# A decoder step on one core: one PSUM bank per unit of the recurrence, earlier decay rows, and key and value weights in 512 KB pieces

## The chip, the core and the metric

The kernel runs on one core of a Trainium2 chip. The core has five engines that run their own queues in order: TensorE (PE in the profile, with its weight loads as PEld), VectorE (DVE), ScalarE (ACT), GpSimd (POOL) and SyncE (SP), which issues nearly all DMA transfers. The metric is device time in microseconds, the median over several executions; lower is better.

## The reference

One inference step of one hybrid decoder layer over 1024 prompt tokens and 8 x 4 sample tokens, all float32, model width 1024. Cut to what matters here:

```python
def hybrid_layer(x, mem_k, mem_v, ssm_h, ...):
    proj = rmsnorm(x, norm_mix) @ w_in                 # z, x/B/C, dt, pool input
    xbc = silu(causal_dwconv(conv_buf, xbc, ...))
    y, ssm_new = ssd_chunked(xs, dt, a, b_ssm, c_ssm, ssm_h)   # 16 heads of 64, state 128
    y = gated_group_rmsnorm(y + xs * ssm_d[:, None], z, ssm_norm)
    pooled = multiscale_pool(...) @ w_pool * pool_scale
    x = x + concat([y, pooled]) @ w_out
    x = x + memory_attention(rmsnorm(x, norm_mem) @ w_mq, mem_k, mem_v) @ w_mo
    return x + conv_gated_mlp(rmsnorm(x, norm_ffn))

def ssd_chunked(x, dt, a, b_in, c_in, h0):             # chunks of 128 tokens
    acs = cumsum(dt * a, within a chunk)
    decay = exp(acs[l] - acs[s]) for s <= l
    y_diag = (C B^T * decay) (x dt)                    # within the chunk
    chunk_states = B^T (exp(acs[-1] - acs) x dt)       # what the chunk adds to the state
    h_next = h * exp(acs[-1]) + chunk_states
    y_off = (exp(acs) C) h                             # from the state before the chunk

def memory_kv(mem, norm_memkv, w_mk, w_mv):            # 256 memory tokens
    hm = rmsnorm(mem, norm_memkv)
    return hm @ w_mk, hm @ w_mv
```

## The kernel before

All prompt and sample tokens (1056 columns) go through each projection together, features on the partitions. Each float32 operand is split into two parts, `hi` and `lo`, and a product is three matmuls (hi x hi, hi x lo, lo x hi). For weights this is done on the fly. A list of `steps` in the order of use loads one piece `[128, 512]` each (256 KB) into a `wr` tile, and `wsplit` makes `wh` on ACT and `wl = wr - wh` on DVE. There are three tiles each of `wr`, `wh` and `wl`. `prep()` runs the next step whenever fewer than two split pieces (units of weights) are ready, and then asks for the loads that stand `AHEAD` = 2 steps further on. A piece is consumed in four blocks of 128 columns.

The stages that matter here follow each other on PE:

1. `w_in`: 28 output tiles, each 8 k-steps of 9 matmuls with 352 columns, into `mm` tiles of three banks (two such tiles, and beside them two `ms` banks of one).
2. In the background of this stage runs the recurrence, a generator that `tick()` advances after each k-step, by one `yield` every `SSD_PACE` = 1.6 ticks (3 at first). Its 32 units are 2 groups x 8 chunks x 2 halves of 4 heads. For a unit, `ssd_load` fetches the decay rows `acs` of its 4 heads, spread over 128 partitions (256 KB), into an `s` tile; `ssd_pre` transposes x into an `ms` bank and multiplies it out into `xd`, and makes `am` (decays times `C B^T`) and `ce` (decayed C) in the tile of the decay rows, by ACT and DVE; `ssd_post`, one unit later, does the output matmuls into an `ms` bank `py` and the state matmul into another `ms` bank `pst`, adds the first to x and the second to the state `hT`. `ssd_group`, once per two units, takes an `ms` bank too. The two `ms` banks are handed out in turn.
3. The samples' recurrence, which loads states `h0T` into `ld` tiles (three tiles of 528 KB), and the pooled half of `w_out` (8 tiles): its inputs come from `scr_pool` through `ld`, and the residual input `xT` is loaded into an `ld` tile for each of the 8 tiles, added and stored to `scr_xp`.
4. Keys and values of the 256 memory tokens: 16 pieces of `w_mk` with 4 x 3 matmuls of 256 columns each, then 16 pieces of `w_mv` with 2 x 3 matmuls of 512 columns each. Meanwhile ACT and DVE finish the gating of the recurrence's output.
5. The recurrence's half of `w_out` (weights `w_out_y`), which loads `scr_xp` into `ld` tiles, and the rest of the layer.

The order of the instructions on each engine is set by a scheduler when the kernel is built, from the program's order and its own idea of durations; at run time each queue is strictly in order. The instructions are recorded through a helper, so the profile has them all at one line, L91 (L92 in the changed kernel), and the names of the tiles tell them apart: `ms<-xd,btm` is the state matmul, `ms<-s,xd` and `ms<-s` are the output matmuls, `ms<-cst,s` the transposes.

Of the kernel before, what the change touches and what calls it, by code (L numbers as in the profile page):

```python
# [10 lines left out]
ALU = mybir.AluOpType  # L11
# [25 lines left out]
VZ = "ppzppzpzpzpzpzzz"  # L37
SSD_EVERY = 3
SSD_PACE = 1.6
SAMPLE_EVERY = 1.5  # L40
GATE_EVERY = 1.5
FOLD_EVERY = 1.2
WINDOWS = (2, 4, 8, 16)
AHEAD = 2
# [34 lines left out]
def body(ctx, tc, A):  # L79
# [20 lines left out]
    V, S, G, PE, DQ = [InOrder(e) for e in (nc.vector, nc.scalar, nc.gpsimd, nc.tensor, nc.sync)]  # L100
# [3 lines left out]
    def dma(out, in_, after=None):  # L104
        d = DQ.dma_start(out, in_)
        after = after or gate[0]
        if after is not None:
            tc.add_manual_dep(d.ins, after.name, NOSYNC, reason="load order")
        return d
# [25 lines left out]
    def pc(name, i, n=1):  # L135
        o = PAR_COLS[name] + i
        return par[:, o:o + n]

    def stile(dt=F32, w=T):
        return sp.tile([P, w], dt, tag="S", name="s")  # L140
# [4 lines left out]
    def ldtile():  # L145
        return lp.tile([P, T], F32, tag="ld", name="ld")
# [4 lines left out]
    def mbtile():  # L151
        return pmm[0].tile([P, 512], F32, tag="mb", name="mb")

    def mstile():
        if pmm[1] is None:
            return mbtile()
        return pmm[1].tile([P, 512], F32, tag="ms", name="ms")
# [15 lines left out]
    steps, sources, issue = [], [], {}  # L173
    ready = deque()
    raws = {}
    at = [0]
# [8 lines left out]
    def load(i):  # L185
        if i in raws:
            return
        src, alloc = sources[i]
        raw = alloc()
        w = 1  # L190
        for d in src.shape[1:]:
            w *= d
        dst = raw[:, :w]
        dma(dst if len(src.shape) == 2 else dst.rearrange("p (k o) -> p k o", k=src.shape[1]), src)
        raws[i] = (raw, w)

    def source(src, step, ahead, alloc=wtile):
        sources.append((src, alloc))
        issue.setdefault(max(0, step - ahead), []).append(len(sources) - 1)
        return len(sources) - 1  # L200
# [8 lines left out]
    def wsplit(raw, w):  # L209
        hi = wp.tile([P, 512], F32R, tag="wh", name="wh")  # L210
        S.activation(hi[:, :w], raw[:, :w], AF.Copy)
        lo = wp.tile([P, 512], F32R, tag="wl", name="wl")
        V.tensor_tensor(lo[:, :w], raw[:, :w], hi[:, :w].bitcast(F32), op=ALU.subtract)
        ready.append((hi, lo, w))

    def plain(i):
        load(i)
        wsplit(*raws[i])

    def plains(srcs):  # L220
        for src in srcs:
            i = source(src, len(steps), AHEAD)
            steps.append(lambda i=i: plain(i))

    def up_part(j, n):
        return A["w_up"][2 * j + 2 - int(n[1]), int(n[2]) - 1]

    def paired(j, names):
# [24 lines left out]
        for n, m, off, alloc in (("s1", "a21", -7, stmp), ("a11", "a11", -4, wtile), ("a21", "a21", -4, stmp),  # L253
                                 ("s4", "a12", 0, stmp), ("a22", "a22", 5, stmp)):
            ids[n] = source(up_part(j, m), n0, -off, alloc)
        for n, x, off in (("s1", up_part(j, "a22"), -5), ("s4", lambda: q["s2"], 1)):
            issue.setdefault(n0 + off, []).append(lambda n=n, x=x: more(n, x))
# [3 lines left out]
        for n in names:  # L261
            if n == "a12":
                plains([up_part(j, "a12")])
            else:
                steps.append(lambda n=n: one(n))

    def down_weights(name, m, c):
        kind = {"t3": 0, "b22": 1, "t1": 2, "t2": 3}
        if name in kind:
# [4 lines left out]
    plains(A["w_in"][m, h] for m in range(28) for h in range(2))  # L274
    plains(scr["wop"][4 * h:4 * h + 4, :, m * P:(m + 1) * P].rearrange("k p o -> p k o")
           for m in range(8) for h in range(2))
    plains(A["w_mk"][m][:, h * 512:(h + 1) * 512] for m in range(8) for h in range(2))
    plains(A["w_mv"][4 * d + k // 2][:, (k % 2) * 512:(k % 2) * 512 + 512] for d in range(2) for k in range(8))
    for nm, n in (("w_out_y", 8), ("w_mq", 8), ("w_mo", 8), ("w_mo", 8), ("w_mo", 7)):
        plains(A[nm][m, h] for m in range(n) for h in range(2))  # L280
    plains(up_part(j, "a12") for j in EARLY)
# [48 lines left out]
    def background(gen, every, bs=bgs):  # L330
        bs.append([gen, 0, every])

    def pace(every):
        if bgs:
            bgs[0][2] = every
# [130 lines left out]
    for b in range(NB):  # L466
        c = slice(b * BW, (b + 1) * BW)
# [205 lines left out]
    for k in range(KT):  # L673
        for pi, x in enumerate((hh[k], hl[k])):
            for b in range(NB):
                PE.matmul(ps[:2 * H, b, :BW], lhsT=wd[:, k].rearrange("p s h -> p (s h)"),
                          rhs=x[:, b * BW:(b + 1) * BW], start=(k == 0 and pi == 0), stop=(k == KT - 1 and pi == 1))
# [12 lines left out]
    def ssd_group(c, g):  # L690
        l = slice(c * P, (c + 1) * P)
        Bf, Cf = xb[8 + g], xb[10 + g]
        ps = mstile()
        PE.transpose(ps[:, 0:P], Bf[:, l], ident)
        PE.matmul(ps[:, P:2 * P], lhsT=Bf[:, l], rhs=Cf[:, l], start=True, stop=True)
        btm = xa.tile([P, P], F32, tag="btm", name="btm", bufs=2)
        S.activation(btm, ps[:, 0:P], AF.Copy)
        cbm = xa.tile([P, P], F32, tag="cbm", name="cbm", bufs=2)
        V.tensor_tensor(cbm, ps[:, P:2 * P], umat, op=ALU.mult)
        grp[g] = (btm, cbm)  # L700

    def ssd_load(c, g, hf):
        h0 = 8 * g + 4 * hf
        at = stile()
        dma(at[:, 0:512].rearrange("p (h l) -> p h l", h=4),
            scr["acs"][h0:h0 + 4, c * P:(c + 1) * P].partition_broadcast(P))
        return at
# [27 lines left out]
    def ssd_post(c, g, hf, am, ce, xd, btm):  # L735
        l = slice(c * P, (c + 1) * P)
        h0 = 8 * g + 4 * hf
        py = mstile()
        for i in range(2):
            o = slice(i * P, (i + 1) * P)  # L740
            for e in range(2):
                PE.matmul(py[64 * e:64 * e + 64, o], lhsT=xd[:, 0, 2 * i + e], rhs=am[:, 2 * i + e],
                          start=True, stop=(c == 0))
            if c > 0:
                for e in range(2):
                    hc = (h0 + 2 * i + e) * 64
                    PE.matmul(py[64 * e:64 * e + 64, o], lhsT=hT[:, hc:hc + 64], rhs=ce[:, 2 * i + e],
                              start=False, stop=True)
        pst = mstile()
        PE.matmul(pst[:, :256], lhsT=btm, rhs=xd[:, 1].rearrange("p h d -> p (h d)"), start=True, stop=True)  # L750
        for i in range(2):
            x = xb[h0 // 2 + i]
            V.scalar_tensor_tensor(x[:, l], x[:, l], pc("ssm_d", h0 // 2 + i), py[:, i * P:(i + 1) * P],
                                   op0=ALU.mult, op1=ALU.add)
        hs = hT[:, h0 * 64:h0 * 64 + 256]
        if c == 0:
            V.tensor_copy(hs, pst[:, :256])
        else:
            hv = hs.rearrange("p (h d) -> p h d", h=4)
            V.tensor_tensor(hv, hv, cd_t[:, c, h0:h0 + 4].unsqueeze(2).to_broadcast([P, 4, 64]), op=ALU.mult)  # L760
            V.tensor_tensor(hs, hs, pst[:, :256], op=ALU.add)
        if c == 7:
            dma(A["o_ssm_p"][:, h0 * 64:h0 * 64 + 256], hs)

# [108 lines left out]
    units = [(c, g, hf) for g in range(2) for c in range(8) for hf in range(2)]  # L873

    def ssd_all():
        loads = {}
        loads[0] = ssd_load(*units[0])
        loads[1] = ssd_load(*units[1])
        yield
        yield  # L880
        pend = None
        for u, un in enumerate(units):
            if un[2] == 0:
                ssd_group(un[0], un[1])
                yield
            nxt = ssd_pre(*un, loads.pop(u))
            yield
            if pend is not None:
                ssd_post(*pend[0], *pend[1])
            if u + 2 < len(units):  # L890
                loads[u + 2] = ssd_load(*units[u + 2])
            yield
            pend = (un, nxt)
        ssd_post(*pend[0], *pend[1])
        yield

    background(ssd_all(), SSD_EVERY)
    for f in XBC_ORDER[6:]:
        xbc_tile(f)
# [43 lines left out]

    pace(SSD_PACE)
    left = {"p": deque(range(8)), "z": deque(range(8))}
    for i, c in enumerate(VZ):
        if "p" not in VZ[i:] and "p" == VZ[i - 1]:
            background(ssd_sample(), SAMPLE_EVERY)
        (pool_tile if c == "p" else z_tile)(left[c].popleft())
# [117 lines left out]
    for d in range(2):  # L1067
        pv = [mbtile() for _ in range(2)]
        for k in range(8):
            whi, wlo, _ = next_unit()  # L1070
            for mt in range(2):
                c = slice(mt * P, (mt + 1) * P)
# [219 lines left out]
    for m in range(8):  # L1292
# [20 lines left out]
        for lb in (1, 0):  # L1313
            src = t[:, lb * 512:(lb + 1) * 512]
# [38 lines left out]
    for c in ATTN:  # L1353
        if c == "s":
            u = len(pts)
# [3 lines left out]
        elif c == "t":  # L1359
            u = len(pt)  # L1360
            pt[u] = attn_tr(pts[u])
        elif c == "o":
            u = min(pt)
# [19 lines left out]
    hs = [None] * 8  # L1383
# [254 lines left out]
    xd = {n: [] for n in xparts}  # L1638
# [108 lines left out]
    for i, name in enumerate(DN_ORDER):  # L1747
# [4 lines left out]
        for m, (c0, c1) in dn_units(name):  # L1752
# [4 lines left out]
            for k in range(c0 // P, c1 // P):  # L1757
# [4 lines left out]
                for b in range(2):  # L1762
                    for pi, (w, h) in enumerate(((whi, 0), (wlo, 0), (whi, TH))):
                        PE.matmul(ps[b][:, :HB], lhsT=w[:, wc], rhs=xt[:, h + b * HB:h + (b + 1) * HB],
                                  start=(first and k == 0 and pi == 0), stop=(k == NH - 1 and pi == 2),
# [14 lines left out]
    xd = xd["b21"]  # L1780
# [3 lines left out]
    for k in range(NH):  # L1784
# [3 lines left out]
        for m in range(4):  # L1788
            wc = slice(m * P, (m + 1) * P)
            for pi, (w, h) in enumerate(((whi, 0), (wlo, 0), (whi, TH))):  # L1790
                PE.matmul(outs[m], lhsT=w[:, wc], rhs=xd[k][:, h:h + LW], start=(k == 0 and pi == 0),
                          stop=(k == NH - 1 and pi == 2))
# [19 lines left out]
    for h in (1, 0):  # L1812
        for i in range(2):
            for m in range(4):
                PE.matmul(o[i][h][:, m * P:(m + 1) * P], lhsT=acc[4 * h + m][:, cs[i]], rhs=ident, start=(m == 0),
                          stop=(h == 1 and m == 3), skip_group_check=True)
# [169 lines left out]
```

## Time and profile before

| | |
|---|---|
| time, median of 3 runs | 1680.94 us (1678.08 to 1685.15) |
| the profiled execution | 1682.67 us, span 1680.9 us |
| granted clock of TensorE | 0.997 |
| PE busy | 1642.8 us (98%) |
| DVE busy | 1180.9 us (70%) |
| ACT busy | 784.4 us (47%) |
| SP's DMA queue, share of 16 engines' span | 54.6%, 289.04 MB |
| moved in all | 306.57 MB, 182 GB/s |

A row of the time line has start and duration in us, engine, operation, the tiles written and read, the shape and a count; in brackets stands how long the engine was idle before, and what ended that. A row of the waits says which engine waited, on what tile, for whom: us in total, times, longest. A row of DMA issues has the count, the size of one, and the median us from issue to landing.

### The profile page before, as it was taken

The page shows a single profiled execution, that of the slowest core. Times are in us where ns is not written, and L with a number is a line of the kernel's source. Part 1 is how long each engine was busy: PE and PEld are TensorE (multiplying, and loading weights), DVE is VectorE, ACT ScalarE, POOL GpSimd, SP SyncE. Part 2 cuts the span into 40 slices and gives each one's busy share as a digit, 9 for nine tenths or more (in the row PEclk, how much of TensorE's full clock was granted, in tenths as well). Part 3 has the DMA queues.
Part 4 walks back from the last instruction along what each step waited for, and adds up shares of the span by engine and source line. Part 5 has one row for each costly group of instructions (what it writes and reads, how often), then busy time and mean ns, then how long its engine had stood idle before and what let it go on. Part 6 is the DMA issues. An engine that isn't in the chain of part 4 may idle for free. (4 is left out here: it accounts for less than half of the span.)

```text
span 1680.9 us, 30585 instructions
## 1 busy us (share of the span) xinstructions
PE 1642.8 (98%) x11808; PEld 1559.3 (93%) x11808; DVE 1180.9 (70%) x1999; ACT 784.4 (47%) x1402; POOL 138.7 (8%) x315
## 2 busy tenths in 40 slices
PE   9999999999999999999999999999999999999998
PEld 8899999899989889999878999999999989999997
DVE  6766768688679576654755896777777878776665
ACT  6565643444514343223533665555544545454451
POOL 0110000001000000000000002232122222100000
PEclk9999999999999999999999999999999999999999
DMA  6243354544696678853666756666566577896542
GB/s 219 85 160 87 66 134 105 111 87 107 224 314 230 192 252 304 301 165 105 233 226 192 228 182 170 177 167 180 145 167 199 168 205 218 284 302 203 159 139 103
DMA packets 187569, 306.57 MB, mean 182 GB/s; under 512 B 43920, under 2 KB 81296, under 8 KB 187424
## 3 DMA queue, kind: packets, MB, share of 16 engines
q1 hardware_dynamic: 178928, 289.04, 54.6%
q0 software_dynamic: 8496, 15.59, 5.6%
q8 instruction: 92, 1.51, 0.4%
q14 instruction: 53, 0.43, 0.1%
HBM read 221.26 MB, written 77.53 MB: 178 GB/s over the span
## 5 line engine op out<-in xcount | busy, mean ns | idle before, releaser
L91 PE MATMUL mb<-s,wh 128*128 128x264 f32 (+4 forms) x4800 | 908.3, 295 | 6.8 <-ACT wh L91 4.7
L91 PEld LDWEIGHTS mb<-s,wh 128*128 128x128 f32 x4800 | 759.5, 189 | 15.1 <-ACT wh L91 5.8
L91 PE MATMUL mb<-s,wl 128*128 128x264 f32 (+4 forms) x2400 | 667.5, 296 | 13.7 <-DVE wl L91 13.3
L91 PEld LDWEIGHTS mb<-s,wl 128*128 128x128 f32 x2400 | 445.8, 189 | 23.6 <-DVE wl L91 20.5
L91 ACT ACTIVATE wh<-wr 128x512 fp32r<-128x512 f32 (+1 forms) x298 | 184.7, 620 | 385.1 <-PE mb L91 177.2
L91 PE MATMUL mm<-s,wh 128*128 128x352 f32 x1728 | 340.9, 330 | 1.5 <-DVE s L91 1.5
L91 PEld LDWEIGHTS mm<-s,wh 128*128 128x128 f32 x1728 | 284.6, 188 | 7.9 <-DVE s L91 2.6
L91 DVE TENSOR_TENSOR wl<-wr,wh 128x512 fp32r<-128x512 f32 (+1 forms) x298 | 201.4, 677 | 109.9 <-ACT wh L91 107.4
L91 PE MATMUL mm<-s,wl 128*128 128x352 f32 x864 | 187.7, 324 | 0.0
L91 DVE SCALAR_TENSOR_TENSOR t<-t,par 128x1104 f32<-128x1104 f32 (+1 forms) x124 | 168.2, 1366 | 26.5 <-ACT t L91 25.4
L91 PEld LDWEIGHTS mm<-s,wl 128*128 128x128 f32 x864 | 147.2, 189 | 1.8 <-issue 1.2
L91 ACT ACTIVATE s<-s 128x512 f32<-128x512 f32 (+7 forms) x117 | 84.2, 730 | 94.2 <-DMA s<-scr_acs 60.7
L91 DVE TENSOR_TENSOR t<-t 128x1024 f32<-128x1024 f32 (+10 forms) x147 | 107.1, 731 | 14.8 <-DMA t<-w_dn 11.1
L91 ACT ACTIVATE wh<-ws 128x512 fp32r<-128x512 f32 x110 | 68.8, 626 | 63.0 <-DMA ws<-w_up 44.9
L91 DVE TENSOR_TENSOR s<-s 128x512 f32<-128x512 f32 (+8 forms) x90 | 74.4, 841 | 30.2 <-ACT s L91 29.8
L91 DVE TENSOR_TENSOR wl<-ws,wh 128x512 fp32r<-128x512 f32 x110 | 75.4, 686 | 21.3 <-ACT wh L91 20.4
L91 ACT ACTIVATE t<-t 128x32 f32<-128x32 f32 (+2 forms) x87 | 46.8, 537 | 88.2 <-DVE t L91 87.7
L91 DVE TENSOR_TENSOR s<-mb,s 128x264 f32<-128x264 f32 (+6 forms) x140 | 61.0, 473 | 30.9 <-PE mb L91 14.9
L91 DVE TENSOR_TENSOR s<-q,s 128x528 fp32r<-128x528 f32 x81 | 56.6, 705 | 36.1 <-ACT s L91 35.7
L91 ACT ACTIVATE t<-t,par 128x1104 f32<-128x1104 f32 (+1 forms) x56 | 73.2, 1307 | 15.5 <-DVE t L91 11.6
L91 ACT ACTIVATE s<-q 128x528 fp32r<-128x528 f32 x81 | 51.9, 643 | 53.7 <-DMA q<-scr_g 50.6
L91 DVE TENSOR_TENSOR ws<-wr,ws 128x512 f32<-128x512 f32 x44 | 30.2, 691 | 57.4 <-issue 31.5
(192 smaller groups left out, 1506.1 us busy)
## 6 DMA issues: line engine op xcount, KB each, us to landing
ws<-w_up SPq DMA_DIRECT2D x88, 256.0 KB, 3.6
q<-scr_g SPq DMA_DIRECT2D x77, 264.0 KB, 3.8
wr<-w_in SPq DMA_DIRECT2D x56, 256.0 KB, 2.9
wr<-w_mo SPq DMA_DIRECT2D x46, 256.0 KB, 3.0
scr_g<-t SPq DMA_DIRECT2D x22, 528.0 KB, 5.2
wr<-w_up SPq DMA_DIRECT2D x44, 256.0 KB, 3.2
s<-scr_acs SPq DMA_DIRECT2D x33, 256.0 KB, 5.1
t<-w_dn SPq DMA_DIRECT2D x32, 256.0 KB, 4.5
```

What stands on the lines that cost most here:

```text
L91: i = fn(*args, **kwargs)
```

## The change

Three edits.

*State part in the output's bank.* `pst` is no longer a bank of its own but the second half of `py`. A unit then takes two `ms` banks where it took three (beside that of `ssd_group`).

*Decay rows four units ahead.* `ssd_load` is called for a unit four units before its use in place of two, and the second half's rows (`hf` = 1) go into an `ld` tile in place of an `s` tile.

*Key and value weights as 512 KB.* `halves` loads a whole `[128, 1024]` row block of `w_mk` or `w_mv` into an `ld` tile, four steps ahead, and splits it in two steps of 512 columns.

```diff
+SSD_AHEAD = 4
...
+    def halves(src):
+        i = source(src, len(steps), 2 * AHEAD, ldtile)
+
+        def half(h):
+            load(i)
+            wsplit(raws[i][0][:, h * 512:(h + 1) * 512], 512)
+
+        steps.extend([lambda: half(0), lambda: half(1)])
...
-    plains(A["w_mk"][m][:, h * 512:(h + 1) * 512] for m in range(8) for h in range(2))
-    plains(A["w_mv"][4 * d + k // 2][:, (k % 2) * 512:(k % 2) * 512 + 512] for d in range(2) for k in range(8))
+    for src in (*(A["w_mk"][m] for m in range(8)), *(A["w_mv"][k] for k in range(8))):
+        halves(src)
...
     def ssd_load(c, g, hf):
         h0 = 8 * g + 4 * hf
-        at = stile()
+        at = ldtile() if (2 * c + hf) % 2 else stile()
...
-        pst = mstile()
-        PE.matmul(pst[:, :256], lhsT=btm, rhs=xd[:, 1].rearrange("p h d -> p (h d)"), start=True, stop=True)
+        pst = py[:, 256:]
+        PE.matmul(pst, lhsT=btm, rhs=xd[:, 1].rearrange("p h d -> p (h d)"), start=True, stop=True)
...
-            V.tensor_copy(hs, pst[:, :256])
+            V.tensor_copy(hs, pst)
...
-            V.tensor_tensor(hs, hs, pst[:, :256], op=ALU.add)
+            V.tensor_tensor(hs, hs, pst, op=ALU.add)
...
-        loads[0] = ssd_load(*units[0])
-        loads[1] = ssd_load(*units[1])
+        for u in range(SSD_AHEAD):
+            loads[u] = ssd_load(*units[u])
...
-            if u + 2 < len(units):
-                loads[u + 2] = ssd_load(*units[u + 2])
+            if u + SSD_AHEAD < len(units):
+                loads[u + SSD_AHEAD] = ssd_load(*units[u + SSD_AHEAD])
```

PE's queue in the recurrence, in the middle of one unit (`ms` with the same number is the same bank in use; in brackets the semaphores that an instruction waits for). Before:

```order
L91 MATMUL ms_2535<-s_2322,xd_2444 64x128 [waits DVE_49]
L91 MATMUL ms_2535<-s_2322,xd_2444 64x128
L91 MATMUL ms_2535<-s_2322,s_1155 64x128 x2
L91 MATMUL ms_2544<-xd_2444,btm_2408 128x256 [waits DVE_49]
L91 MATMUL mm_2416<-s_182,wh_2417 128x352 x3
```

And now:

```order
L92 MATMUL ms_2529<-s_2152,xd_2439 64x128 [waits DVE_49,PE_49]
L92 MATMUL ms_2529<-s_2152,xd_2439 64x128
L92 MATMUL ms_2529<-s_2152,s_1155 64x128 x2
L92 MATMUL ms_2529<-xd_2439,btm_2403 128x256
L92 MATMUL mm_2411<-s_182,wh_2412 128x352 x3
```

The state matmul has lost its wait for DVE: it goes into the bank of the output matmuls.

DVE's queue where it takes up one unit's output (`s_1155` is the state, `dtp` its decay, `par` holds `ssm_d`). Before:

```order
L91 SCALAR_TENSOR_TENSOR s_999<-s_999,par_74,ms_2307 128x128 [waits PE_49]
L91 TENSOR_TENSOR t_2254<-t_2254,t_2244 128x16 [waits DVE_49]
L91 SCALAR_TENSOR_TENSOR s_1152<-s_1152,par_74,ms_2307 128x128
L91 TENSOR_TENSOR s_1155<-s_1155,dtp_92 128x256
L91 TENSOR_TENSOR s_2226<-s_2226,s_549 128x512 [waits Activation_49]
L91 TENSOR_TENSOR s_1155<-s_1155,ms_2316 128x256 [waits DVE_49,PE_49]
```

And now:

```order
L92 TENSOR_TENSOR s_1155<-s_1155,dtp_92 128x256 [waits PE_49]
L92 TENSOR_TENSOR t_2251<-t_2251,t_2241 128x16 [waits DVE_49]
L92 SCALAR_TENSOR_TENSOR s_999<-s_999,par_74,ms_2304 128x128 [waits PE_49]
L92 SCALAR_TENSOR_TENSOR s_1152<-s_1152,par_74,ms_2304 128x128
L92 TENSOR_TENSOR s_1155<-s_1155,ms_2304 128x256 [waits DVE_49]
```

The state's decay stands ahead of the two output additions, and the state's addition no longer waits for PE: the first output addition has waited for both.

SP's queue at the end of the pooled projection. Before:

```order
L91 DMA scr_xp_80<-ld_5322 128x1056 [waits DMAHW4_49,DVE_49]
L91 DMA wr_5435<-w_mk 128x512 [waits DVE_49]
L91 DMA ld_6225<-scr_xp_80 128x1056 [waits DMAHW6_49,DMAHW4_49]
L91 DMA wr_5482<-w_mk 128x512 [waits DMAHW7_49,DVE_49,Activation_49]
L91 DMA scr_xp_80<-ld_5426 128x1056 [waits DMAHW0_49,DVE_49]
L91 DMA wr_5545<-w_mk 128x512 [waits DMAHW1_49,DVE_49,Activation_49]
L91 DMA ld_6337<-scr_xp_80 128x1056 [waits DMAHW2_49,DMAHW0_49]
```

And now:

```order
L92 DMA scr_xp_80<-ld_5292 128x1056 [waits DMAHW4_49,DVE_49]
L92 DMA wr_6029<-w_out_y 128x512 [waits DVE_49]
L92 DMA ld_5396<-xT 128x1056 [waits DMAHW6_49,DMAHW4_49]
L92 DMA wr_6041<-w_out_y 128x512 [waits DMAHW7_49,DVE_49,Activation_49]
L92 DMA scr_xp_80<-ld_5396 128x1056 [waits DMAHW6_49,DMAHW0_49,DVE_49]
L92 DMA ld_5450<-w_mk 128x1024 [waits DMAHW1_49,DMAHW0_49]
L92 DMA ld_5499<-xT 128x1056 [waits DMAHW2_49,DVE_49]
L92 DMA scr_xp_80<-ld_5499 128x1056 [waits DMAHW3_49,DMAHW2_49,DVE_49]
L92 DMA ld_5535<-w_mk 128x1024 [waits DVE_49]
L92 DMA ld_5576<-w_mk 128x1024 [waits DMAHW5_49,DMAHW3_49]
```

The last two `xT` loads now stand between key tiles, the last of them waiting for DVE (the first key tile's splits); pieces of `w_out_y` stand where pieces of `w_mk` stood; and the `scr_xp` loads have left this place.

## The prediction, made before the changed kernel had run

> **What bounds the kernel now.** I read the page's busy shares, then busy time by stretch, the waits of the two stretches that the change touches, and the time line there.
>
> ```profile
> span 1680.9 us, 30585 instructions
> PE 1642.8 (98%) x11808; PEld 1559.3 (93%) x11808; DVE 1180.9 (70%) x1999; ACT 784.4 (47%) x1402; POOL 138.7 (8%) x315
> ```
>
> TensorE (PE) is busy for 98% of the span, so only time in which PE stands can be won: 1680.9 - 1642.8 = 38 us in all. The stretches (us; then busy time and instructions of PE, PEld, DVE, ACT, POOL; clock; DMA share; GB/s) show how much of it lies here:
>
> ```profile
> 195.00:425.00 230.00, 224.53 (x1639) 209.94 (x1638) 176.52 (x374) 93.33 (x165) 5.67 (x19) 1.00 0.48 108
> 440.00:500.00 60.00, 59.47 (x397) 50.99 (x396) 43.19 (x71) 13.86 (x18) 0.00 (x0) 1.00 0.88 297
> 525.00:552.00 27.00, 27.00 (x171) 26.65 (x170) 21.86 (x26) 8.72 (x10) 0.00 (x0) 1.00 0.48 169
> 552.00:604.00 52.00, 48.99 (x304) 41.75 (x303) 34.18 (x57) 23.25 (x36) 0.00 (x0) 1.00 0.62 196
> ```
>
> The recurrence (195 to 425 us) leaves PE idle for 230.0 - 224.5 = 5.5 us, keys and values (552 to 604) for 52.0 - 49.0 = 3.0 us. The other two rows are neighbours that I use below. The clock is full everywhere. In the recurrence the waits are
>
> ```profile
> ACT s L91 <- DMA s<-scr_acs: 62.3, 24, 4.9
> DVE s L91 <- ACT s L91: 36.4, 19, 4.5
> PEld ms L91 <- DVE xd L91: 7.5, 9, 1.8
> PE ms L91 <- DVE xd L91: 5.3, 5, 1.6
> ```
>
> ACT loses 62 us to the decay rows and hands 36 us on to DVE, but only 5.3 us reach PE, in five places, and all of them name `xd`. One of the five:
>
> ```profile
> 216.47 0.38 PE L91 MATMUL ms<-cst,s 128*128 128x128 f32 x2
> ...
> 219.65 0.44 PE L91 MATMUL ms<-s,xd 128*64 128x128 f32 x4
> ...
> 220.29 0.63 ACT L91 ACTIVATE s<-s 128x512 f32<-128x512 f32 x1 [4.93 <-DMA s<-scr_acs]
> ...
> 220.95 0.69 DVE L91 TENSOR_TENSOR s<-s 128x512 f32<-128x512 f32 x1 [4.55 <-ACT s L91]
> 221.56 0.68 DVE L91 TENSOR_TENSOR xd<-ms,dtp 128x512 f32<-128x512 f32 x1
> ...
> 222.30 0.70 PE L91 MATMUL ms<-xd,btm 128*128 128x256 f32 x2 [1.55 <-DVE xd L91]
> ...
> 223.46 0.42 DVE L91 TENSOR_TENSOR s<-s,dtp 128x256 f32<-128x256 f32 x1
> ```
>
> PE transposes the next unit's x at 216.47. DVE could read them out, but stands behind a multiplication that waits for ACT, which waits 4.9 us for decay rows. The state matmul at 222.30 needs no result of this `xd`: its operands are a unit older. It wants the `ms` bank from which this `xd` is read, since there are two such banks and it takes one of its own. So the late load and the third bank per unit make one stall together; either edit alone should end it.
>
> In the stretch of keys and values:
>
> ```profile
> PEld mb L91 <- DVE wl L91: 3.5, 7, 1.0
> PEld mb L91 <- ACT wh L91: 3.0, 3, 1.4
> ```
> ```profile
> PE mb L91 <- ACT wh L91: 2.0, 2, 1.0
> PE mb L91 <- DVE wl L91: 1.0, 3, 0.5
> ```
> ```profile
> ACT wh L91 <- DMA wr<-w_mk: 7.5, 7, 2.9
> ACT wh L91 <- DMA wr<-w_mv: 5.6, 3, 2.7
> ```
>
> PE waits for split weights, and the splits for the 256 KB loads.
>
> **State part in the output's bank: 5.3 us won.** No instruction goes: 32 state matmuls stay, without their wait on DVE. Each `ms` bank is now asked for again one step of the generator later than before. A step takes about what lies between 216.47 and 219.65 above, 3.2 us; `xd` was done at 222.24, 5.8 us after its transposes, and the bank's next user now comes two steps, 6.4 us, after them. So even the late `xd` just fits. What it costs: the two DVE instructions that add `ssm_d` times x to the output now also wait for the state matmul, 0.70 us of PE each (row at 222.30). 32 x 0.70 = 22 us is the most DVE could lose; it has 230.0 - 176.5 = 53 us of idle time there, and the decay of the state (223.46, 0.42 us), which needs neither, is put ahead of them. I take nothing; both ends stay: 0 and, if DVE's lateness reached PE as it did before, 5.3 us of new stalls.
>
> On this the Trainium skill ("PSUM — Partial Sum Buffer", section "PSUM bank collisions raise a hardware error") speaks against the edit: accesses must be kept apart by bank and quadrant, whatever the address, so output and state in one bank wait for each other. The order of the changed program agrees with it (these two wait for the state matmul); by this page alone the sum would be without the 5.3 us.
>
> **Decay rows four units ahead: nothing beyond that.** The same 32 loads, asked for earlier.
>
> ```profile
> s<-scr_acs SPq DMA_DIRECT2D x33, 256.0 KB, 5.1
> ...
> L91 DVE TENSOR_TENSOR xd<-ms,dtp x32: 682/684/692, 149.0 to 410.9; 128x512 f32<-128x512 f32 x32
> ```
>
> A unit takes (410.9 - 149.0) / 31 = 8.4 us, so two more units are 17 us against a landing of 5.1 us: ACT's 62 us and most of DVE's 36 us go. Both engines stay far below PE (93 and 177 of 230 us), so what they win is idle time; it only makes the 5.3 us sure. Every second unit now takes an `ld` tile, so the first state of the samples and the first pooled tiles, which had sat in `ld` from early on, load later, behind the last unit's decay rows. That request and the first split of a pooled tile:
>
> ```profile
> 397.70 0.37 SPq L91 DMA_DIRECT2D s<-scr_acs  x1
> ...
> 428.60 1.07 ACT L91 ACTIVATE s<-ld 128x1056 fp32r<-128x1056 f32 x1
> ```
>
> That leaves 30 us for two waits on a unit's end (8.4 us each) and a load of some 5 us: nothing. Two more activation table loads appear on ACT, hidden by its idle time.
>
> **Key and value weights as 512 KB: 2.0 us won.** 32 loads of 256 KB become 16 of 512 KB; bytes, splits and matmuls stay. What changes is the ring. PE's first two units, and one of the stalls:
>
> ```profile
> 552.38 0.40 PE L91 MATMUL mb<-s,wh 128*128 128x256 f32 x2
> ...
> 553.79 0.40 PE L91 MATMUL mb<-s,wh 128*128 128x256 f32 x2
> ...
> 562.87 2.04 ACT L91 ACTIVATE wh<-wr 128x512 fp32r<-128x512 f32 x3 [2.88 <-DMA wr<-w_mk]
> 563.53 0.69 DVE L91 TENSOR_TENSOR wl<-wr,wh 128x512 fp32r<-128x512 f32 x1 [2.81 <-ACT wh L91]
> ```
>
> A unit is 553.79 - 552.38 = 1.41 us, and three `wr` tiles turn in 4.2 us. Of that the issue takes 0.3 and the two splits 0.7 each (2.04 / 3 and 0.69), so a landing may take 2.5 us; the rows below have 3.3 and 3.0, hence the stalls. Three `ld` tiles of two units each turn in 8.5 us; issue, the second half's wait of 1.41 and its splits take 3.1, so a landing may take 5.4 us.
>
> ```profile
> wr<-w_mk SPq DMA_DIRECT2D x16, 256.0 KB, 3.3
> wr<-w_mv SPq DMA_DIRECT2D x16, 256.0 KB, 3.0
> ld<-h0T SPq DMA_DIRECT2D x8, 512.0 KB, 4.1
> ld<-kc SPq DMA_DIRECT2D x9, 512.0 KB, 6.4
> ld<-xT SPq DMA_DIRECT2D x8, 528.0 KB, 5.0
> scr_xp<-ld SPq DMA_DIRECT2D x8, 528.0 KB, 3.4
> ```
>
> 512 KB lands in 4.1 us (`h0T`) to 6.4 us (`kc`). I take 4.1 to 5: `h0T` is the same form into the same tiles, mostly from 440 to 500 us, where the DMA engines are busier (0.88) than here (0.62). Then the ring keeps pace, and the 3.0 us go. At 6.4 us it would lose (6.4 - 5.4) x 16 / 3 = 5.3 us instead.
>
> The start costs something. `ld` is shared with the last tiles of the pooled projection, and the eighth `xT` load now waits until the first key tile is split:
>
> ```profile
> 546.94 0.69 DVE L91 TENSOR_TENSOR wl<-wr,wh 128x512 fp32r<-128x512 f32 x1 [0.59 <-ACT wh L91]
> 552.57 1.26 DVE L91 TENSOR_TENSOR ld<-mm,ld 128x1056 f32<-128x1056 f32 x1 [4.95 <-PE mm L91]
> 553.75 0.68 DVE L91 TENSOR_TENSOR wl<-wr,wh 128x512 fp32r<-128x512 f32 x1
> ```
>
> The split ends at 547.6, the load lands 5.0 us later near 553, the addition slips by 0.4 us, and the split at 553.75 with it; that one was done at 554.4 and PE wants it two units after 552.38, at 555.2. The fourth key tile waits for the second's splits (two units after 552.38, 555.2) and lands near 560; the fifth waits for the addition's store (554.5 + 3.4) and lands near 562.5. PE wants them at about 561 and 564, less 1.4 us for splitting: 0 to 1 us late each. I charge 1.0 us together, with 0 and 2 as ends. The queue meanwhile holds nothing that PE needs sooner: three tiles of `w_out_y` are asked for earlier than before, in the idle `wr` tiles, and the `scr_xp` loads that move behind the last value tile are first read a tile of 72 matmuls later.
>
> **Sum:** 5.3 + 3.0 - 1.0 = 7.3 us. The profiled execution took 1682.7 us, 1.7 above the median of 1680.9; so 1675.4 for it, and 1673.6 for the median.
>
> **Rivals.** *All of it and more.* PE's idle time counts only from a modelled end. By the rows of the weight loads the same waits are 7.5 and 3.5 + 3.0 us, 14 together. If these are the true losses and the start is free, 8.5 to 14 us go: 1667 to 1672.4, middle 1670. For it: each PE wait ends with a weight load that waited longer. Against: a quarter of the forecast's gain is a ring that barely turns fast enough.
>
> *The stall moves (the page's rule).* The additions held by the state matmul make DVE late, the next transposes wait for their bank, and the decay rows' gain is eaten; or keys and values start late. Gain 0 to 4 us: 1677 to 1681. Against it stands the doubled distance between two users of a bank. The page named above is the rule behind this.
>
> *Slower.* 512 KB lands too slowly. Past 5.4 us each further us costs 16 / 3 = 5.3 us; the 7.3 us are used up at 5.4 + 7.3 / 5.3 = 6.8 us, and the kernel is 8.4 us slower at 8.4 us. `kc` reached 6.4 in its median, under other traffic; at 8.4 us the time is 1689.3.
>
> **How the numbers follow.** About 0.5%, 8.4 us, is what a measurement of this kernel can tell from no change. The forecast (gain 4 to 8.4 us, 1672.5 to 1677) gets 0.48, all of it and more 0.36, the moved stall 0.10, slower 0.06, of which half stays within 0.5%. So faster 0.36, same 0.61, slower 0.03. The time is the forecast's, 1673.6. The range goes to 1667.5 below, which takes in most of the second case, and to 1681 above, which takes in the moved stall.
>
> **What would show it.** Right: in the recurrence no `PE ms <- DVE xd`, ACT's wait for `scr_acs` below 10 us, PE idle below 1 us; in keys and values 16 loads landing in 4 to 5.5 us and PE idle of about 1 us. Wrong: a new row of PE's waits naming `s`, `cbm` or `ld` in the recurrence, `ACT wh <- DMA ld<-w_mk` of several us, or idle PE time before 552 us while the last addition waits for `xT`.

## The result, and the profile after

The changed kernel took 1671.5 us (median of 5 runs, 1666.7 to 1672.2) against 1681.8 us of the kernel before (5 runs, 1678.1 to 1685.2). The ratio is 0.993, with a 95% interval of 0.9916 to 0.9945, so 9 to 14 us less: faster by more than 0.5%. The forecast was 1673.6 us. The time lies in its range, but inside the span of the rival "all of it and more" (1667 to 1672.4) and just outside the forecast's own (1672.5 to 1677); the forecast had given that rival a chance of 0.36 and itself 0.48.

The page of the changed kernel, and its busy time by stretch (columns as in the prediction):

```profile
span 1664.9 us, 30518 instructions
PE 1637.7 (98%) x11808; PEld 1559.9 (94%) x11808; DVE 1181.4 (71%) x1999; ACT 786.1 (47%) x1404; POOL 144.3 (9%) x315
```
```profile
195.00:425.00 230.00, 229.53 (x1675) 215.14 (x1674) 175.94 (x374) 91.08 (x161) 5.67 (x19) 1.00 0.50 110
525.00:552.00 27.00, 27.00 (x183) 27.00 (x182) 20.93 (x23) 9.54 (x12) 0.00 (x0) 1.00 0.46 162
552.00:604.00 52.00, 52.00 (x326) 47.75 (x325) 39.53 (x62) 25.14 (x39) 0.00 (x0) 1.00 0.76 245
```

PE's idle time fell from 5.5 to 0.5 us in the recurrence and from 3.0 to 0.0 us in keys and values. Fixed windows understate what that is worth, because the work moves under them: in the same 52 us PE now runs 326 matmuls instead of 304. I therefore measure a stretch from its first to its last matmul. The instructions of PE by tile, with the first and last start, of the kernel before:

```profile
L91 PE MATMUL ms<-xd,btm x64: 377/379/484, 162.7 to 417.0; 128*128 128x256 f32 x64
L91 PE MATMUL mb<-s,wh x4800: 274/285/505, 552.4 to 1636.1; 128*128 128x264 f32 x140, 128*128 128x352 f32 x30, 128*128 128x272 f32 x11, 128*128 128x256 f32 x6
L91 PE MATMUL mb<-wh,s x64: 387/396/504, 577.7 to 605.0; 128*128 128x512 f32 x64
```

and of the changed kernel:

```profile
L92 PE MATMUL ms<-xd,btm x64: 379/431/484, 162.3 to 410.9; 128*128 128x256 f32 x64
L92 PE MATMUL mb<-s,wh x4800: 274/285/500, 546.1 to 1620.3; 128*128 128x264 f32 x140, 128*128 128x352 f32 x30, 128*128 128x272 f32 x11, 128*128 128x256 f32 x6
L92 PE MATMUL mb<-wh,s x64: 389/393/497, 568.9 to 592.7; 128*128 128x512 f32 x64
```

The state matmuls (`ms<-xd,btm`) span the recurrence: 254.3 us before, 248.6 now. The first key matmul (first of `mb<-s,wh`) to the last value matmul with the weights' `hi` part (last of `mb<-wh,s`) spans keys and values: 605.0 - 552.4 = 52.6 before, 592.7 - 546.1 = 46.6 now. That is 5.7 + 6.0 = 11.7 us, inside the 9 to 14 us of the interval. Each length is that of one execution; that the sum meets the middle of the interval (11.8) so closely is in part luck.

The same two lengths for every kernel that ran, one profiled execution each, with what lies between them, what lies behind (to the last matmul), and PE's waits for `xd` in the recurrence, in us:

| kernel | recurrence | between | keys and values | rest | waits for `xd` |
|---|---|---|---|---|---|
| before | 254.3 | 135.4 | 52.6 | 1069.1 | 5.3 |
| changed | 248.6 | 135.2 | 46.6 | 1065.4 | 0.5 |
| e1, bank alone | 251.7 | 136.4 | 52.6 | 1071.5 | 2.8 |
| e2, rows ahead alone | 253.7 | 135.6 | 52.3 | 1068.9 | 5.5 |
| e3, 512 KB alone | 256.5 | 136.8 | 46.6 | 1069.9 | 6.9 |
| e4, bank and 512 KB | 252.1 | 135.6 | 46.6 | 1071.4 | 3.3 |
| e5, two loads per tile | 248.7 | 137.4 | 46.6 | 1067.7 | 0.5 |
| e6, 256 KB in `ld` | 248.9 | 135.5 | 52.6 | 1066.9 | 0.7 |
| e7, ring of two | 249.2 | 136.0 | 47.7 | 1069.6 | 0.9 |
| e8, no rows loaded | 247.9 | 135.4 | 51.9 | 1071.8 | 0 |
| e9, two ahead, `ld` kept | 249.1 | 137.4 | 46.6 | 1071.3 | 0.9 |

The recurrence follows PE's waits for `xd`: length less wait is 247.9 to 249.6 us in all eleven. The rest scatters by 6.4 us with the same program text; keys and values take 46.6 us in all five kernels whose ring holds six units and 51.9 to 52.6 us in all five with a ring of three units. A profiled span is therefore no measure of one stage, its own length is. (The profiled execution of the changed kernel is also its shortest, 4.8 us under its median; the 3.7 us in its last column are no gain of the change.)

The waits of the changed kernel from 195 to 425 us:

```profile
ACT ld L92 <- DMA ld<-scr_acs: 45.2, 11, 5.0
DVE ld L92 <- ACT ld L92: 21.6, 8, 4.5
ACT s L92 <- DMA s<-scr_acs: 19.4, 10, 2.9
DVE s L92 <- PE ms L92: 10.3, 19, 3.2
...
DVE s L92 <- ACT s L92: 5.8, 3, 4.6
...
PEld ms L92 <- DVE xd L92: 1.2, 3, 0.8
...
PE ms L92 <- DVE xd L92: 0.5, 1, 0.5
```

PE's waits for `xd` are gone but for one. ACT's waits for decay rows are not: 45.2 + 19.4 = 64.6 us, where they were 62.3. In keys and values (552 to 604 us, and just so 545 to 595) no row of PE is left, and the loads land, from issue to data in place, in

```profile
ld<-w_mk SPq DMA_DIRECT2D x8, 512.0 KB, 4.3
ld<-w_mv SPq DMA_DIRECT2D x8, 512.0 KB, 4.3
```

### The profile page after: what moved, and what is told of

It is laid out like the page before. It is cut to its first block, busy times and chain, and to the rows that moved or that the text cites. A ratio compares the mean times of both kernels' runs of the same rounds, so it can differ in the third digit from the quotient of the medians.

```text
span 1664.9 us, 30518 instructions
## 1 busy us (share of the span) xinstructions
PE 1637.7 (98%) x11808; PEld 1559.9 (94%) x11808; DVE 1181.4 (71%) x1999; ACT 786.1 (47%) x1404; POOL 144.3 (9%) x315
## 5 line engine op out<-in xcount | busy, mean ns | idle before, releaser
L92 ACT ACTIVATE wh<-wr 128x512 fp32r<-128x512 f32 (+1 forms) x266 | 164.5, 619 | 361.4 <-PE mb L92 166.5
L92 DVE TENSOR_TENSOR wl<-wr,wh 128x512 fp32r<-128x512 f32 (+1 forms) x266 | 179.4, 675 | 100.3 <-ACT wh L92 99.2
L92 ACT ACTIVATE s<-s 128x512 f32<-128x512 f32 (+7 forms) x87 | 65.1, 763 | 29.3 <-DMA s<-scr_acs 19.4
L92 DVE TENSOR_TENSOR s<-s 128x528 fp32r<-128x528 f32 (+8 forms) x76 | 64.8, 872 | 6.2 <-ACT s L92 5.7
L92 PE MATMUL mb<-s 128*128 128x256 f32 (+2 forms) x414 | 68.9, 323 | 0.0
```

The lines of the kernel that those rows point to most:

```text
L92: i = fn(*args, **kwargs)
```

## The experiments

My theory after the result: in the recurrence a late load makes `xd` late, and a third bank per unit makes PE ask for its bank early; in keys and values the ring of three 256 KB tiles turned too slowly. Rivals: one of the two edits of the recurrence does it alone; the larger transfer as such, and not the ring, wins in keys and values.

### The three edits apart

e1 has the `py[:, 256:]` edit alone, e2 `SSD_AHEAD = 4` with every second unit's rows in `ld`, e3 `halves`, e4 the first and the third.

> Only the state part in the output's bank. Theory A (the third bank per unit makes the stall, whatever makes xd late): PE's wait for xd in the recurrence falls from 5.3 us to under 1 us though ACT still waits some 60 us for decay rows; keys and values keep their waits (about 3.0 us on PE); time 5 to 6 us under before, ratio about 0.9968. Theory B (the late decay rows are the cause, the bank only passes it on): new waits for s or cbm of 3 us or more appear on PE, gain under 3 us.

> Only the decay rows, asked for four units ahead. My prediction (either edit alone ends the stall): PE's wait for xd under 1 us, time 5 us under before, ratio about 0.997. Theory A, after the trace of the changed kernel, in which ACT still waits 65 us for decay rows because it just runs further ahead: DVE is still held behind ACT, so PE's wait for xd stays between 3 and 6 us and the time is within 2 us of before.

> Only the 512 KB key and value tiles. Theory A (the three-tile ring of 256 KB turned too slowly; PE lost 6 us there, of which the profile's idle time shows 3): the stage of keys and values is 6 us shorter, no PE wait over 0.3 us in it; the recurrence keeps 5.3 us of waits for xd; time 6 us under before, ratio about 0.9965. Theory B (the gain there was lent by the earlier recurrence): 3 us or less.

> Bank and 512 KB tiles, decay rows two units ahead as before. Theory A (the earlier rows add nothing): as the full change, 10 to 12 us under before, ratio about 0.993, PE's wait for xd under 1 us. Theory B (the earlier rows carry part of it): 3 us or more behind the full change, with PE waits in the recurrence.

Measured, against 1685.3 us of the kernel before:

| kernel | us | ratio | 95% interval |
|---|---|---|---|
| e1 | 1680.0 | 0.9961 | 0.9946 to 0.9976 |
| e2 | 1684.8 | 0.9991 | 0.9974 to 1.0008 |
| e3 | 1681.1 | 0.9975 | 0.9959 to 0.9992 |
| e4 | 1677.4 | 0.9935 | 0.9914 to 0.9955 |

Keys and values are plain: 46.6 us with 512 KB pieces, 52.6 (52.3) without, whatever the recurrence does. The recurrence needs both edits. The bank alone saves 2.6 us (254.3 to 251.7; 4.4 between e3 and e4, 256.5 to 252.1) and leaves PE 2.8 and 3.3 us of waits for `xd`; the rows ahead alone save 0.6 and leave 5.5; both together save 5.7, and in all five kernels with the bank and the `ld` tiles at most 0.9 us of these waits is left.

That the two win more than their sum is not shown: 5.7 stands against 2.6 + 0.6, but the old recurrence took 254.3 us in one kernel and 256.5 in another (e3), and the times of the whole kernels add up (0.9961 x 0.9991 x 0.9975 = 0.9927; the change had 0.993). Nor do the times tell e4 from the whole change (0.9935 against 0.993), and e1's 4 to 9 us are more than the 2.6 us of its profiled execution, which took 2.9 us above e1's median. The split between the edits stands on the lengths and the waits. By these e2 and e3 came out as theory A had it; e1 kept more of the waits than theory A allowed, without the new ones of theory B; e4 kept waits as in theory B, though its ratio is that of theory A.

The waits in e1 and then in e2, 195 to 425 us:

```profile
ACT s L91 <- DMA s<-scr_acs: 71.6, 23, 6.4
...
PE ms L91 <- DVE xd L91: 2.8, 3, 1.5
```
```profile
ACT ld L92 <- DMA ld<-scr_acs: 48.1, 11, 5.4
...
ACT s L92 <- DMA s<-scr_acs: 17.5, 9, 2.9
...
PE ms L92 <- DVE xd L92: 5.5, 4, 2.3
```

In none of them does ACT stop waiting for rows. One place, the same unit in four kernels, shows how the two edits work together. Time line of the kernel before:

```profile
247.25 0.39 SPq L91 DMA_DIRECT2D s<-scr_acs  x1
249.38 0.38 PE L91 MATMUL ms<-cst,s 128*128 128x128 f32 x2
...
253.90 0.68 DVE L91 TENSOR_TENSOR xd<-ms,dtp 128x512 f32<-128x512 f32 x1
254.64 0.70 PE L91 MATMUL ms<-xd,btm 128*128 128x256 f32 x2 [0.98 <-DVE xd L91]
```

of e2 (rows ahead alone):

```profile
245.04 0.39 SPq L92 DMA_DIRECT2D ld<-scr_acs  x1
...
247.84 0.38 PE L92 MATMUL ms<-cst,s 128*128 128x128 f32 x2
...
252.70 0.68 DVE L92 TENSOR_TENSOR xd<-ms,dtp 128x512 f32<-128x512 f32 x1
...
253.44 0.70 PE L92 MATMUL ms<-xd,btm 128*128 128x256 f32 x2 [1.32 <-DVE xd L92]
```

of e1 (bank alone):

```profile
246.81 0.39 SPq L91 DMA_DIRECT2D s<-scr_acs  x1
247.14 0.38 PE L91 MATMUL ms<-cst,s 128*128 128x128 f32 x2
...
251.35 0.70 PE L91 MATMUL ms<-xd,btm 128*128 128x256 f32 x2
...
254.21 0.68 DVE L91 TENSOR_TENSOR xd<-ms,dtp 128x512 f32<-128x512 f32 x1
...
254.95 0.33 PE L91 MATMUL ms<-cst,s 128*128 128x128 f32 x1 [1.46 <-DVE xd L91]
```

and of the changed kernel:

```profile
244.43 0.39 SPq L92 DMA_DIRECT2D ld<-scr_acs  x1
...
247.32 0.38 PE L92 MATMUL ms<-cst,s 128*128 128x128 f32 x2
...
250.73 0.63 ACT L92 ACTIVATE ld<-ld 128x512 f32<-128x512 f32 x1 [4.28 <-DMA ld<-scr_acs]
...
251.39 0.69 DVE L92 TENSOR_TENSOR ld<-ld,s 128x512 f32<-128x512 f32 x1 [4.22 <-ACT ld L92]
...
251.53 0.70 PE L92 MATMUL ms<-xd,btm 128*128 128x256 f32 x2
...
252.00 0.68 DVE L92 TENSOR_TENSOR xd<-ms,dtp 128x512 f32<-128x512 f32 x1
...
253.52 0.27 PE L92 MATMUL ms<-cst,s 128*128 128x128 f32 x1
```

Counted from the transposes (`ms<-cst,s ... x2`), with PE's wish being its start less the wait in brackets:

| | rows asked for | `xd` done | PE wants the bank |
|---|---|---|---|
| before | -2.1 | 5.2 | 4.3, state matmul |
| e2 | -2.8 | 5.5 | 4.3, state matmul |
| e1 | -0.3 | 7.8 | 6.4, `ssd_group`'s transpose |
| changed | -2.9 | 5.4 | 6.2, `ssd_group`'s transpose |

The shared bank moves PE's wish from 4.3 to 6.2 or 6.4 us. An `xd` at 5.2 to 5.5 us misses the first and meets the second. But once PE runs on, the rows come later in its time (e1: asked for at -0.3), `xd` slips to 7.8 and misses again; the additional tiles bring the request back to -2.9. In the changed kernel DVE still stands 4.2 us for the row and reaches `xd` only behind it; what has changed is that the deadline lies later and the row is asked for in time to meet it.

### Why asking earlier does not end the wait, and what the late rows cost

Nothing lets the rows come early. The order of DVE's queue in the changed kernel has this piece:

```
L92 TENSOR_TENSOR s_2472<-s_2472,s_549 128x512 [waits Activation_49]
L92 TENSOR_TENSOR xd_2439<-ms_2436,dtp_92 128x512 [waits PE_49]
```

`xd_2439` belongs to the unit whose rows are in `s_2152`; after it come `ld_2223`, `s_2318`, `ld_2389` and `s_2472`. So the multiplication ahead of this `xd` is that of the unit four later. In the kernel before it is that of the next unit (`s_2478` ahead of `xd_2507`, whose rows are `s_2394`). The scheduler has moved the instructions that use the rows ahead as far as the load, and their wait stands ahead of `xd` as before.

e8 takes the late rows away, in the kernel before; e9 undoes the distance in the program but keeps the `ld` tiles:

```diff
 # e8, on the kernel before
-        dma(at[:, 0:512].rearrange("p (h l) -> p h l", h=4),
-            scr["acs"][h0:h0 + 4, c * P:(c + 1) * P].partition_broadcast(P))
+        V.memset(at[:, 0:512], 0.0)
 # e9, on the changed kernel
-SSD_AHEAD = 4
+SSD_AHEAD = 2
```

> The kernel before, but the 32 transfers of decay rows are left out: DVE sets each unit's rows to zero in their place (the recurrence's values are then others; 32 DVE instructions of 128x512 more). The bank of its own for the state matmul stays. If late rows alone make `xd` late and so PE wait: PE's waits for `xd` in the recurrence fall from 5.3 us to under 1 us, first to last state matmul takes 248.5 to 250 us as in the changed kernel instead of 254.3, and the kernel takes 4 to 6 us less than before. Rival, that three banks per unit in a ring of two make PE wait even for an `xd` that is in time: 3 us or more of those waits stay, 252 us or more.

> The changed kernel, but decay rows are asked for two units ahead as before the change; every second unit's rows still go into an `ld` tile. The program's distance is undone, the additional buffers stay, and the order on PE is the same. If the number of buffers sets how early the rows are fetched (the scheduler takes a load as soon as its tile is free): as the changed kernel, under 1 us of PE waiting for `xd` in the recurrence, 1671 to 1673 us. Rival, that the program's distance does it: as the bank edit alone, about 3 us of PE waiting for `xd`, some 1674 us.

e8's stretch from 195 to 425 us:

```profile
195.00:425.00 230.00, 230.00 (x1680) 215.93 (x1678) 189.84 (x407) 93.14 (x170) 5.67 (x19) 1.00 0.30 81
```

PE is never idle there, although the state matmul has its own bank: three banks per unit cost nothing when `xd` is in time. So without late rows there is no stall; the early deadline only adds to it (e1, with a later one, has less of it though ACT waits longer for rows). The stall is worth 254.3 - 247.9 = 6.4 us, and the change got 5.7 of them. (e8 took 1675.3 us against 1686.5, ratio 0.9928, 0.9911 to 0.9944, so 9 to 15 us, more than the 6.4 + 0.7 us that the two stretches show. The two profiled executions, 1678.0 and 1682.7 us, differ by only 4.7, so their stretches cannot show where the remainder lies; it stays open. The transfers left out also take 8 MB off the queue.)

e9 took 1671.4 us (ratio 0.9924, 0.9902 to 0.9946), its recurrence 249.1 us, its waits:

```profile
ACT ld L92 <- DMA ld<-scr_acs: 48.4, 11, 5.1
ACT s L92 <- DMA s<-scr_acs: 20.5, 10, 3.3
...
PE ms L92 <- DVE xd L92: 0.9, 1, 0.9
```

That is the changed kernel: beside the `ld` tiles the number 4 does nothing that these lengths show. The three more tiles do: e9 differs from e4 only in them, and the recurrence goes from 252.1 to 249.1 us. The scheduler puts a load where its tile comes free (in SP's queue nearly all of these loads wait for PE, which reads the tile's last content). In e9, too, the multiplication of the unit four later stands ahead of `xd`, though the program asks two ahead.

### Keys and values: ring or transfer

All three stand on the changed kernel. e5 fills each 512 KB tile by two transfers, e6 puts one 256 KB piece into each `ld` tile, e7 holds one of the three `ld` tiles.

```diff
 # e5, in load(), for ld tiles
+            for h in range(2):
+                dma(dst[:, h * 512:(h + 1) * 512], src[:, h * 512:(h + 1) * 512])
 # e6, what halves() does instead
+        for h in range(2):
+            i = source(src[:, h * 512:(h + 1) * 512], len(steps), AHEAD, ldtile)
+            steps.append(lambda i=i: plain(i))
 # e7, around the key and value loops
+    held = ldtile()
+    G.memset(held[:, :8], 0.0)
...
+    G.tensor_copy(held[:, 8:16], t[:, 512:520])
```

> The changed kernel, but each 512 KB `ld` tile of key or value weights is filled by two transfers of 256 KB. It keeps the ring (three tiles of two units) and takes away the larger transfer. Ring theory: as the changed kernel, no wait of PE for `wh` or `wl` in keys and values, 1671 to 1673 us. Rival, that fewer and larger transfers made the gain: the 6 us of this stage are lost again, about 1677.5 us, and the waits for the landing stand in the rows as before the change.

> The changed kernel, but key and value weights go as single 256 KB pieces into the three `ld` tiles, asked for two steps ahead, so that the ring is three units deep as before and each tile half empty. Ring theory: PE waits again for `wh` and `wl`, about 3 us idle in its own rows and some 6 us by the stage's length, 1677 to 1678 us. Rival, that what counted was moving the loads out of the `wr` tiles (free for `w_out_y`) and into others: no waits, 1671.5 us.

> The changed kernel, but one `ld` tile is held through keys and values, so that two tiles of 512 KB turn. Ring theory: two units take 2.8 us, two tiles turn in 5.6 us, less the 3.1 us of issue, second half and splits leaves 2.5 us for a landing of 4.3 us; 1.8 us late at every second of 16 tiles, some 14 us, 1685 us; with half of it hidden 1678 us. Rival, that the ring's depth does not bind: under 1 us, 1671 to 1673 us.

Against 1684.5 us: e5 1673.9 us (ratio 0.9936, 0.9911 to 0.9961), e6 1676.1 (0.995, 0.9931 to 0.9969), e7 1674.8 (0.9936, 0.9912 to 0.996). The times alone hardly separate them; the stretch does.

e5 keeps 46.6 us with 256 KB transfers and has no wait of PE there: the size of a transfer is not the cause. e6 has 52.6 us again, with the loads in the new tiles. Its waits, 545 to 602 us:

```profile
ACT wh L92 <- DMA ld<-w_mv: 11.6, 9, 3.1
...
PEld mb L92 <- DVE wl L92: 4.8, 10, 1.0
PEld mb L92 <- ACT wh L92: 2.1, 4, 0.8
PE mb L92 <- DVE wl L92: 1.3, 4, 0.6
...
PE mb L92 <- ACT wh L92: 1.0, 2, 0.6
```

PE's rows say 2.3 us and the weight loads' 6.9; the stretch is 6.0 us longer. So what counts is how many units the ring holds: three are too few for these landings, six are enough. (e6 also asks two steps ahead in place of four. A ring of three units leaves no room for four, so the depth and the distance are not told apart.)

e7 was expected at some 14 us and cost 1.1. One turn of a tile in it, on the time line:

```profile
564.31 0.33 SPq L92 DMA_DIRECT2D ld<-w_mk  x1
...
567.85 1.15 ACT L92 ACTIVATE wh<-ld 128x512 fp32r<-128x512 f32 x2 [1.54 <-DMA ld<-w_mk]
568.51 1.29 DVE L92 TENSOR_TENSOR wl<-ld,wh 128x512 fp32r<-128x512 f32 x2 [1.07 <-ACT wh L92]
569.83 3.10 SPq L92 DMA_DIRECT2D ld<-w_mv  x2
```

From the issue at 564.31 to the next into the same tile, at 569.83 when both its halves are split, are 5.5 us, and PE uses two tiles in 4 x 1.41 = 5.6. My budget had charged 1.41 us for the second half's wait; a tile that comes late has none, since both halves are split at once (1.95 us, 567.85 to 569.80). The landings were 3.7 and 3.5 us, shorter than the 4.3 that I had reckoned with. The ring theory stands by e5 and e6; its price for a ring of two was mine and wrong.

## Why the prediction was right or wrong

**State part in the output's bank, 5.3 us: 2.6 to 4.4 by itself.** Both edits of the recurrence together won 5.7 us, near the 5.3 + 0 of their two terms, but the split was wrong, and that the two errors cancel is luck. The step "either edit alone should end it" failed: the bank alone won 2.6 to 4.4 us, the rows 0.6. I had measured the deadline (6.4 us; the unit above shows 6.2 to 6.4) against an `xd` of 5.8 us that was late under the old waits. In e1, with the deadline moved, PE is ahead of the loads and `xd` is at 7.8. That the edit costs nothing on DVE was right: with the bank alone DVE's waits for PE in `ms` (`DVE s <- PE ms`) are 3.2 and 2.8 us (e1, e4), against 6.7 before. In the changed kernel they are 10.3, but e2 (8.4) and e8 (19.4) have more than before with the old banks, so the growth is not the bank's; none of it reached PE. The Trainium skill's rule on banks ("PSUM — Partial Sum Buffer", section "PSUM bank collisions raise a hardware error") is agreed with in that the additions do wait: in the changed kernel one starts at 244.65, behind its state matmul (243.91 to 244.61), and its counterpart in the kernel before at 246.09, within its state matmul (245.97 to 246.67). The lost gain that I drew from the rule did not come.

**Decay rows four units ahead, nothing: wrong both ways.** "ACT's 62 us and most of DVE's 36 us go" failed: 64.6 us of ACT remain, and 21.6 + 5.8 of DVE. The distance between two calls in the program is not the distance on the chip when a scheduler moves the user along with the load. And the edit is not nothing: beside the bank it is worth 3.1 to 3.5 us (251.7 and 252.1 to 248.6), by the profiled executions, and through its tiles, not its number.

**Keys and values, 2.0 us: the mis-sized term; 6.0 measured.** The landing (4.1 to 5 us; 4.3) and the ring's budget were right in direction. Two sizes failed. The start was charged 1.0 us and cost nothing: "between" is 135.4 and 135.2 us, and from the first key matmul on PE has no wait, while ACT waits only 2.4 us for key tiles. And the loss before was 6.0, not 3.0: I took PE's idle row, which counts from an end that the profile models. The weight loads' rows (3.5 + 3.0) had it, and so had my own ring: the budget of 2.5 us against landings of 3.3 and 3.0 is (0.8 + 0.5) x 16 / 3 = 6.9 us. I used that formula for the rival and not for the kernel before.

**The rivals.** "All of it and more" gave the time, for the larger part of its reason: the start was free, and the weight loads' rows were the measure in keys and values (6.5 against 6.0). In the recurrence the loss (6.4 us by e8) lies between PE's row (5.3) and theirs (7.5), and the change did not win all of it. The moved stall and the slow landing did not come. A version that beats the changed kernel is not in sight in these stages: 0.7 us are left of e8's recurrence, and PE has no wait in keys and values.

## What to carry to other kernels

Measure a stage by its first and last matmul, and estimate a ring's loss as (landing + issue + splits - turn) x turns, with only those waits that a late tile really has: it gave 6.9 us for 6.0 here, and 14 for 1.1 where a wait was charged that a late tile does not have. PE's idle row showed half of the loss or less (3.0 and 2.3 us of 6.0). Asking for a load earlier helps only if something lets it land earlier (a free buffer), and only if the instruction that waits for it does not move ahead with it; look at what stands behind that instruction in its queue. Two edits of one stall are to be measured apart and together: here neither ended it alone, and together they did.

## What the hardware showed that I had not expected

The landing of one and the same load differs from kernel to kernel. In the median, 512 KB of `w_mk` and of `w_mv` landed in 4.3 and 4.3 us in the changed kernel and in e4, in 3.7 and 3.7 in e3, in 3.9 and 3.4 in e9, all with three tiles turning, and in 3.7 and 3.5 with two (e7); as two 256 KB transfers it landed in 3.8 and 3.2 us each (e5). So no effect of the ring's depth on the landing shows, and a budget needs slack: the stage took 46.6 us in all of the first four. And the stall of the recurrence was not the same in kernels with the old banks: PE waited 5.3 us for `xd` before, 5.5 in e2 and 6.9 in e3, whose recurrence has the same program text as before (254.3, 253.7 and 256.5 us). I take it that this hangs on the moment at which a load lands; no run shows it.
